# Strassen on part of the last feed-forward product of a decoder layer, with its weight sums made in DRAM

## The chip, the cores and the metric

The kernel runs on one core of one Trainium2 chip. The time is the device time of one launch in microseconds (us). The engines are PE (TensorE: matrix products), ACT (ScalarE), DVE (VectorE), POOL (GpSimd) and SP (SyncE, which here only issues transfers). The core's 16 DMA engines move data between DRAM and the on-chip memory SBUF; matrix products accumulate in PSUM.

## The reference

One decoder layer on 512 tokens of width 1024, in float32, with post-normalisation and a residual weight alpha = 2^0.25:

```python
h = _layernorm(ALPHA * h + 0.5 * _swiglu(h, w_ffn1_in, w_ffn1_out), ln1_g, ln1_b)
h = _layernorm(ALPHA * h + _parallel_mixer(h, w_mix_in, ...), ln2_g, ln2_b)
h = _layernorm(ALPHA * h + _memory_attention(h, mem, xa_wq, xa_wk, xa_wv, xa_wo), ln3_g, ln3_b)
h = _layernorm(ALPHA * h + 0.5 * _swiglu(h, w_ffn2_in, w_ffn2_out), ln4_g, ln4_b)

def _swiglu(h, w_in, w_out):
    gate, up = jnp.split(h @ w_in, 2, axis=-1)
    return (jax.nn.silu(gate) * up) @ w_out
```

The feed-forward width is 2816, so that a second product contracts over 2816 (22 tiles of 128, "k-tiles") and has 512 × 1024 results. The attention has 4 heads and attends to 256 memory tokens.

## The kernel before, in words

**Precision.** Every float32 operand is split into two parts of a shorter type that PE reads faster: ACT copies it into the high half (`split`, L65), DVE subtracts that from the operand and gets the low half (L66). A product is three matmuls: high × high, high × low, low × high.

**Weights.** A weight is read in blocks of 128 × 1024 float32 (512 KB, covering two k-tiles and half of the output columns). `wblock` (L69 to L78) has SP load a block into a buffer `raw_...` (seven of these), ACT cast it into `whi_...`, and DVE make `wlo_...`. Blocks that stay until the end of a product lie in larger buffers `ws_...`.

**Stages.** First feed-forward (f1), the mixer, its output product (mo), the memory keys (weights wk), the memory values (wv, 8 blocks of 12 matmuls, L655 to L671), for each head the queries (wxq, two blocks), scores, softmax and values, the output product of the attention (xo), and the second feed-forward (f2). The first products of the feed-forwards already use Strassen's scheme with seven products (L322). Their second products go through `out_gemm`: for each half of the columns, all 22 k-tiles, four token tiles and three matmuls, 528 in all (L210 to L212, results f2ps, left sides f2gs made from the activations f2g). `ln_tile` then normalises a token tile; POOL computes one column `rstd` for it (L165).

**Order.** A scheduler sets the order within each engine from the order of the program and the buffers; at run time each engine takes its instructions strictly in that order and waits with semaphores. All loads stand in one queue, SP's. POOL has little to do: between the last rstd of mo and the first of xo, nothing.

Of the kernel before, what the change touches and what calls it, by code (L numbers as in the profile page):

```python
# [21 lines left out]
FF = 2816  # L22
FT = FF // P
# [3 lines left out]
ALPHA = 2.0 ** 0.25  # L27
LN_EPS = 1e-5
# [5 lines left out]
def layer_kernel(ctx: ExitStack, tc: tile.TileContext, a, out):  # L34
    nc = tc.nc
# [3 lines left out]
    res = ctx.enter_context(tc.tile_pool(name="res", bufs=1))  # L39
    sm = ctx.enter_context(tc.tile_pool(name="sm", bufs=6))  # L40
    st = ctx.enter_context(tc.tile_pool(name="st", bufs=4))
    psum = ctx.enter_context(tc.tile_pool(name="psum", bufs=6, space=bass.MemoryType.PSUM))

    def b8(shape, dt, name):
        return big.tile(shape, dt, tag="b8", name=name)

    def mm_ps(name):
        return psum.tile([P, 512], F32, tag="mm", name=name)
# [15 lines left out]
    def split(src, hi, lo):  # L64
        nc.scalar.copy(out=hi, in_=src)  # L65
        nc.vector.tensor_tensor(out=lo, in0=src, in1=hi.bitcast(F32), op=ALU.subtract)  # L66


    def wblock(src, name, stay=False):  # L69
        raw = raw4([P, 1024], f"raw_{name}")  # L70
        nc.sync.dma_start(raw, src)
        if stay:
            both = b8([P, 2, 1024], F32R, f"ws_{name}")
            hi, lo = both[:, 0, :], both[:, 1, :]
        else:
            hi, lo = q4([P, 1024], f"whi_{name}"), q4([P, 1024], f"wlo_{name}")
        split(raw, hi, lo)
        return hi, lo  # L78
# [31 lines left out]
    first = [(ps0[0], ps0[1]), (ps0[2], ps0[3])]  # L110
# [17 lines left out]
    xT = [(xt[k // 2][:, k % 2, 0, :], xt[k // 2][:, k % 2, 1, :]) for k in range(KT)]  # L128
# [18 lines left out]
    mhalf = const.tile([P, 4], F32, name="mhalf")  # L147
    nc.vector.memset(mhalf, -0.5)
    h = [res.tile([P, D], F32, name=f"h{t}") for t in range(NT)]


    def ln_bcast(g, b):
        G, B = raw4([P, D], "G"), raw4([P, D], "B")
        nc.sync.dma_start(G, g.partition_broadcast(P))
        nc.sync.dma_start(B, b.partition_broadcast(P))
        return G, B

    def ln_tile(t, stats, GB, eps):
        G, B = GB
        mv = st.tile([P, 2], F32, tag="mv", name="mv")  # L160
        nc.vector.bn_aggr(mv, stats)
        ve = st.tile([P, 1], F32, tag="ve", name="ve")
        nc.vector.tensor_scalar(ve, mv[:, 1:2], eps, None, op0=ALU.add)  # L163
        rstd = st.tile([P, 1], F32, tag="rstd", name="rstd")
        nc.gpsimd.tensor_tensor(out=rstd, in0=ve, in1=mhalf[:, 0:1], op=ALU.pow)  # L165
        for hf in range(2):
            sl = slice(hf * 512, hf * 512 + 512)
            nc.vector.scalar_tensor_tensor(
                out=h[t][:, sl], in0=h[t][:, sl], scalar=mv[:, 0:1], in1=G[:, sl],
                op0=ALU.subtract, op1=ALU.mult)  # L170
            nc.vector.scalar_tensor_tensor(
                out=h[t][:, sl], in0=h[t][:, sl], scalar=rstd, in1=B[:, sl],
                op0=ALU.mult, op1=ALU.add)

    def transpose_h(t, tiles, ys=None):
        if ys is not None:
            if t % 2 == 0:
                ys.append(b8([P, 2, KT, P], F32, f"y{t // 2}"))
        for hf in range(2):
            ps = tr_ps(f"trh{t}{hf}")  # L180
            for j in range(4):
                k = hf * 4 + j
                nc.tensor.transpose(ps[:, j * P:(j + 1) * P], h[t][:, k * P:(k + 1) * P], ident)  # L183
            pv = ps.rearrange("p (a b n) -> p a b n", a=2, b=2)
            for q in range(2):
                T = tiles[hf * 2 + q]
                tsl = slice(t * P, (t + 1) * P)
                split(pv[:, q], T[:, :, 0, tsl], T[:, :, 1, tsl])
            if ys is not None:
                nc.scalar.copy(out=ys[t // 2][:, t % 2, hf * 4:hf * 4 + 4, :], in_=ps.rearrange("p (k n) -> p k n", k=4))  # L190
# [51 lines left out]
        return [(tiles[k // 2][:, k % 2, 0, :], tiles[k // 2][:, k % 2, 1, :]) for k in range(KT)]  # L242


    def proj_T(w, X, n=S, name="pj"):
        hi, lo = w
        ps = mm_ps(name)
        for k in range(KT):
            wsl = slice(k * P, (k + 1) * P)
            mm3(ps[:, :n], hi[:, wsl], lo[:, wsl], X[k][0], X[k][1], k == 0, k == KT - 1)  # L250
        return ps[:, :n]
# [14 lines left out]
    RIGHT = {"a11": "b11", "a12": "b21", "s1": "t1", "s2": "t2", "s3": "t3", "s4": "b22", "a22": "t4"}  # L266
    BANK = {"a11": "u", "s2": "u", "s3": "u", "a22": "u", "s1": "v", "s4": "v", "a12": "w"}

    def ffn(win, wout, xT, todo, g, b, name, final, first=None, lead=2, pre=None, ws0=None):
        gt = [b8([P, 4, S], F32, f"{name}g{q}") for q in range(-(-FT // 4))]  # L270
        raws, quads, ps, sg, c22 = {}, {}, {}, {}, {}
        X = quarters_of(xT)
# [33 lines left out]
        lo, hi = slice(0, 256), slice(256, 512)  # L306
# [60 lines left out]
        for gi in range(0, len(order), 2):  # L367
# [13 lines left out]
            if not final and 4 <= gi < 4 + 2 * NT:  # L381
                t = gi // 2 - 2
                nc.sync.dma_start(h[t], a["x"][t * P:(t + 1) * P, :])
        for j in order[-2:]:
            product(j, "a22")

        gs = {}

        def act(k):
            if k // 2 not in gs:  # L390
# [11 lines left out]
             pre=lambda: wf.extend(wblock(a["wmix"][FF_ + hd], f"wf{hd}") for hd in range(2)))  # L402
# [50 lines left out]
    for hd in range(H):  # L453
        ps = tr_ps("dg")
# [75 lines left out]
    for li, m in enumerate(LEVELS):  # L530
# [6 lines left out]
        for g in range(2):  # L537
            ps = tr_ps(f"lv{m}")
# [49 lines left out]
    for c in range(NT - 1):  # L588
        cs = slice(c * P, (c + 1) * P)
        ps = tr_ps("krt")  # L590
# [24 lines left out]
    for c in range(NT):  # L615
        cs = slice(c * P, (c + 1) * P)
        ps = mm_ps("o")
# [6 lines left out]
        o = sm.tile([P, S], F32, tag="sg", name="o")  # L624
        for hd in range(H):
# [6 lines left out]
                                in0=ps.rearrange("p (h d) -> p h d", h=H),  # L632
                                in1=rs.unsqueeze(2).to_broadcast([P, H, P]), op=ALU.mult)
# [3 lines left out]
    for c, o in enumerate(os_):  # L637
        cs = slice(c * P, (c + 1) * P)
        pt = tr_ps("ot")
        for hd in range(H):  # L640
# [4 lines left out]
            out=og.rearrange("p (h d) -> p h d", h=H), in0=pt.rearrange("p (h d) -> p h d", h=H),  # L645
            scalar=gn[:, 0:1], in1=GS[:, :, cs], op0=ALU.mult, op1=ALU.mult)
# [6 lines left out]

    for k in range(3, KT):
        mem_key(k)  # L655
    VM = [b8([P, 2, D], F32R, f"VM{q}") for q in range(2)]
    for hf in range(2):
        ps = [mm_ps(f"vm{hf}{t}") for t in range(2)]
        for blk in range(4):
            hi, lo = wblock(a["wv"][hf, blk], f"wv{hf}{blk}")  # L660
            for t in range(2):
                tsl = slice(t * P, (t + 1) * P)
                for j in range(2):
                    k = blk * 2 + j
                    wsl = slice(j * 512, (j + 1) * 512)
                    nc.tensor.matmul(ps[t], mT[k][0][:, tsl], hi[:, wsl], start=k == 0, stop=False)
                    nc.tensor.matmul(ps[t], mT[k][0][:, tsl], lo[:, wsl], start=False, stop=False)
                    nc.tensor.matmul(ps[t], mT[k][1][:, tsl], hi[:, wsl], start=False, stop=k == KT - 1)
# [74 lines left out]
    ys, wx = [], []  # L743
    X3 = out_gemm(a["wo"], KT, lambda k: (OT[k // 2][:, k % 2, 0, :], OT[k // 2][:, k % 2, 1, :]),
                  ALPHA, a["ln3_g"], a["ln3_b"], LN_EPS, "xo", ys=ys,
                  pre=lambda: wx.extend(wblock(a["w2in"][u * FT], f"f2{'gu'[u]}0") for u in range(2)))


    ffn(a["w2in"], a["w2out"], X3, lambda: sums_tiles(ys), a["ln4_g"], a["ln4_b"], "f2", True, ws0=wx)


def _cols(w):
# [68 lines left out]
```

## Time and profile before

| | |
|---|---|
| median of three runs | 1080.48 us (1080.31 to 1081.1) |
| the profiled execution's own time | 1082.22 us |
| its span, first to last instruction | 1080.3 us |
| busy: PE / DVE / ACT / POOL | 1066.6 / 732.4 / 456.2 / 40.2 us |
| mean granted PE clock | 0.996 of full speed |
| read from DRAM / written | 110.67 / 2.10 MB |

How to read it: all times within the execution are microseconds from the span's start. A row of a timeline gives the start, the duration, the engine, the line of the code, the operation, the tile written and those read, and the count, with the idle time before it and what ended that in brackets. A row of windows gives the stretch, its length, the busy time and count of each engine, the granted PE clock, the mean busy share of the 16 DMA engines, and GB/s. "PEld" is PE's loading of the stationary operand, which runs beside its matmuls. A row of the list of waits gives the engine and what it wrote, the engine waited for, total us, times and the longest.

### The profile page before, as it was taken

How to read it: one execution, taken by the hardware profiler on the slowest of the kernel's cores; microseconds unless marked ns; L12 is line 12 of the kernel's file. 1: busy time of each engine (PE TensorE's matmuls, PEld its weight loads, DVE VectorE, ACT ScalarE, POOL GpSimd, SP SyncE). 2: the span in 40 equal slices, each digit the busy share in tenths (PEclk: the TensorE clock that was granted, in tenths of full speed). 3: DMA queues.
4: the chain of work that ended last, by engine and by line, in shares of the span. 5: the costliest groups of instructions: out<-in, count | busy, mean ns of one | idle time of the engine just before them, and what ended most of it. 6: DMA issues, size and time to landing. Idle time of an engine off the chain costs nothing. (4 is left out here: it accounts for less than half of the span.)

```text
span 1080.3 us, 17019 instructions
## 1 busy us (share of the span) xinstructions
PE 1066.6 (99%) x6758; PEld 966.0 (89%) x6758; DVE 732.4 (68%) x1316; ACT 456.2 (42%) x810; POOL 40.2 (4%) x54
## 2 busy tenths in 40 slices
PE   9999999999999999999999999999999999999997
PEld 8899999998888888889889988888999999988885
DVE  7999878884425733675777456589987888882516
ACT  5666555572221332223415344335555555561300
POOL 0000000000000020411000000010000000000001
PEclk9999999999999999999999999999999999999999
DMA  9243233263341322222415521301323323443302
GB/s 359 72 136 100 89 111 114 80 188 105 106 139 56 99 62 91 71 80 79 156 39 195 153 82 40 128 29 59 118 79 118 118 79 117 135 124 98 133 1 78
DMA packets 34495, 113.87 MB, mean 105 GB/s; under 512 B 4336, under 2 KB 5616, under 8 KB 34416
## 3 DMA queue, kind: packets, MB, share of 16 engines
q1 hardware_dynamic: 34416, 112.78, 32.3%
q8 instruction: 53, 0.87, 0.3%
q14 instruction: 26, 0.21, 0.1%
HBM read 110.67 MB, written 2.10 MB: 104 GB/s over the span
## 5 line engine op out<-in xcount | busy, mean ns | idle before, releaser
L66 DVE TENSOR_TENSOR wlo_f<-raw_f,whi_f 128x1024 fp32r<-128x1024 f32 x38 | 46.5, 1223 | 85.7 <-PE f1ps L211 39.9
L65 ACT CAST whi_f<-raw_f 128x1024 fp32r<-128x1024 f32 x38 | 40.0, 1052 | 103.1 <-PE f2ps L212 46.5
L322 PE MATMUL f2u<-xt,qf2s 128*128 128x256 f32 x480 | 61.8, 284 | 0.7 <-DVE f2sg L336 0.7
L322 PE MATMUL f1u<-xt,qf1s 128*128 128x256 f32 x480 | 61.5, 284 | 0.0
L322 PEld LDWEIGHTS f2u<-xt,qf2s 128*128 128x128 f32 x480 | 59.1, 192 | 1.9 <-issue 1.9
L322 PEld LDWEIGHTS f1u<-xt,qf1s 128*128 128x128 f32 x480 | 59.4, 193 | 0.4 <-ACT qf1s L65 0.4
L210 PE MATMUL f1ps<-whi_f,f1gs 128*128 128x512 f32 x152 | 59.3, 390 | 0.0
L211 PE MATMUL f1ps<-wlo_f,f1gs 128*128 128x512 f32 x152 | 59.2, 389 | 0.0
L211 PE MATMUL f2ps<-wlo_f,f2gs 128*128 128x512 f32 x152 | 59.2, 389 | 0.0
L210 PE MATMUL f2ps<-whi_f,f2gs 128*128 128x512 f32 x152 | 59.1, 389 | 0.0
L212 PE MATMUL f1ps<-whi_f,f1gs 128*128 128x512 f32 x152 | 59.0, 391 | 0.0
L212 PE MATMUL f2ps<-whi_f,f2gs 128*128 128x512 f32 x152 | 58.8, 390 | 0.0
L165 POOL TENSOR_TENSOR rstd<-ve,mhalf 128x1 f32<-128x1 f32 x16 | 14.4, 900 | 685.4 <-DVE ve L163 685.4
L322 PE MATMUL f1v<-xT,qf1s 128*128 128x256 f32 x240 | 32.2, 291 | 2.1 <-ACT qf1s L65 2.1
L212 PEld LDWEIGHTS f2ps<-whi_f,f2gs 128*128 128x128 f32 x152 | 28.5, 188 | 6.1 <-DVE f2gs L66 0.3
L212 PEld LDWEIGHTS f1ps<-whi_f,f1gs 128*128 128x128 f32 x152 | 28.5, 188 | 6.0 <-DVE f1gs L66 0.3
L211 PEld LDWEIGHTS f2ps<-wlo_f,f2gs 128*128 128x128 f32 x152 | 28.5, 188 | 6.0
L210 PEld LDWEIGHTS f2ps<-whi_f,f2gs 128*128 128x128 f32 x152 | 28.5, 188 | 5.9
L211 PEld LDWEIGHTS f1ps<-wlo_f,f1gs 128*128 128x128 f32 x152 | 28.5, 188 | 5.9
L210 PEld LDWEIGHTS f1ps<-whi_f,f1gs 128*128 128x128 f32 x152 | 28.5, 188 | 5.8
L322 PEld LDWEIGHTS f1v<-xT,qf1s 128*128 128x128 f32 x240 | 30.8, 199 | 2.5 <-ACT qf1s L65 2.3
L322 PE MATMUL f1u<-xT,qf1a 128*128 128x256 f32 x240 | 32.1, 283 | 0.0
(337 smaller groups left out, 2957.1 us busy)
## 6 DMA issues: line engine op xcount, KB each, us to landing
raw_f<-in_w1out SPq DMA_DIRECT2D x22, 512.0 KB, 3.9
raw_f2g<-in_w2in SPq DMA_DIRECT2D x22, 512.0 KB, 3.8
raw_f2u<-in_w2in SPq DMA_DIRECT2D x22, 512.0 KB, 4.1
raw_f<-in_w2out SPq DMA_DIRECT2D x22, 512.0 KB, 3.7
raw_f1g<-in_w1in SPq DMA_DIRECT2D x20, 512.0 KB, 4.1
raw_f1u<-in_w1in SPq DMA_DIRECT2D x20, 512.0 KB, 4.4
raw_wk<-in_wk SPq DMA_DIRECT2D x8, 512.0 KB, 4.6
raw_mo<-in_wmixo SPq DMA_DIRECT2D x8, 512.0 KB, 3.6
```

What stands on the lines that cost most here:

```text
L65: nc.scalar.copy(out=hi, in_=src)
L66: nc.vector.tensor_tensor(out=lo, in0=src, in1=hi.bitcast(F32), op=ALU.subtract)
L165: nc.gpsimd.tensor_tensor(out=rstd, in0=ve, in1=mhalf[:, 0:1], op=ALU.pow)
L210: nc.tensor.matmul(ps[t], ah[:, tsl], wh, start=i == 0 and j == 0, stop=False)
L211: nc.tensor.matmul(ps[t], ah[:, tsl], wl, start=False, stop=False)
L212: nc.tensor.matmul(ps[t], al[:, tsl], wh, start=False, stop=i == nb - 1 and j == 1)
L322: nc.tensor.matmul(o, q[:, w, wsl], x[k][r], start=opens and k == 0 and n == 0, stop=ends and k == 3 and n == 2, skip_group_check=True)
```

## The change

The last feed-forward's second product is computed by another scheme on 16 of its 22 k-tiles. The contraction's first 16 k-tiles and the 1024 columns are cut in two, as are the tokens, and seven products of half sizes stand for eight: 28 blocks × 12 matmuls. The six k-tiles left are done as before (144 matmuls), accumulating into the same PSUM banks. Three of the seven right sides are blocks of the weight itself; four are sums t1 to t4 of blocks. These sums are built in a scratch area of DRAM: for each of four block rows SP issues four DRAM-to-DRAM copies of 512 KB, and POOL four accumulating transfers (t1 += w, t3 += w, t2 += t1, t4 += t2). The calls stand in the loop over the wv blocks, after every second one; a hint puts each copy after SP's latest weight load, and each accumulate after POOL's latest rstd. The left sums are made by DVE from the activations (`combine`).

```diff
+    scr = ctx.enter_context(tc.tile_pool(name="scr", bufs=1, space=bass.MemoryType.DRAM))
...
+    last = [None, None]
     def wblock(src, name, stay=False):
         raw = raw4([P, 1024], f"raw_{name}")
-        nc.sync.dma_start(raw, src)
+        last[0] = nc.sync.dma_start(raw, src).ins
...
-        nc.gpsimd.tensor_tensor(out=rstd, in0=ve, in1=mhalf[:, 0:1], op=ALU.pow)
+        last[1] = nc.gpsimd.tensor_tensor(out=rstd, in0=ve, in1=mhalf[:, 0:1], op=ALU.pow).ins
...
+    class Sums:
+        def __init__(self, wsrc, name):
+            self.w, self.name, self.T, self.todo = wsrc, name, {}, []
+            for b in range(4):
+                for p, hf, kb in (("t1", 0, b), ("t3", 1, b), ("t2", 1, b + 4), ("t4", 0, b + 4)):
+                    self.todo.append((p, b, hf, kb))
+        def copy(self, n):
+            for p, b, hf, kb in self.todo[:n]:
+                T = self.T[p, b] = scr.tile([P, 1024], F32, name=f"{self.name}{p}{b}")
+                with tc.issue_after(last[0]):
+                    nc.sync.dma_start(T, self.w[hf, kb])
+                if p == "t4":
+                    for o, x in (("t1", self.w[1, b]), ("t3", self.w[1, b + 4]), ("t2", self.T["t1", b]), ("t4", self.T["t2", b])):
+                        with tc.issue_after(last[1]):
+                            nc.gpsimd.dma_start(self.T[o, b], x, accum_op=ALU.add, max_dma_last_dim=8192)
+            del self.todo[:n]
+
+    def strassen_gemm(wsrc, gt, S_, alpha, g, b, eps, name, final, pre):
...
+        def left(p):
+            T = []
+            for i in range(2):
+                t = b8([P, 4, 2, 256], F32R, f"{name}{p}{i}")
+                split(quarter_[p][i], t[:, :, 0, :], t[:, :, 1, :])
+                T.append(t)
+            return T
+        def combine(o, x, y, op):
+            for i in range(2):
+                nc.vector.tensor_tensor(out=quarter_[o][i], in0=quarter_[x][i], in1=quarter_[y][i], op=op)
+        def right(p):
+            direct = {"b11": (0, 0), "b21": (0, 4), "b22": (1, 4)}
+            for i in range(4):
+                src = wsrc[direct[p][0], direct[p][1] + i] if p in direct else S_.T[p, i]
+                yield wblock(src, f"{name}{p}{i}")
+        def product(T, p, ps, opens, ends):
+            for i, (wh, wl) in enumerate(right(p)):
+                for j in range(2):
+                    k = 2 * i + j
+                    csl = slice(j * 512, (j + 1) * 512)
+                    for t in range(2):
+                        tsl = slice(t * P, (t + 1) * P)
+                        ah, al = T[k // 4][:, k % 4, 0, tsl], T[k // 4][:, k % 4, 1, tsl]
+                        for n, (x, y) in enumerate(((ah, wh), (ah, wl), (al, wh))):
+                            nc.tensor.matmul(ps[t], x, y[:, csl], ...)
...
+        L = left("a11")
+        product(L, "b11", u, True, False)
+        combine("s1", "a21", "a22", ALU.subtract)
+        L = left("s1")
...   (products t1, t2, b21, t3, b22, t4 in the same manner, with their additions into h)
+        ws = [[wblock(wsrc[hf, kb], f"{name}{hf}_{kb}", stay=hf == 0 or kb < 10) for kb in range(8, FT // 2)]
+              for hf in range(2)]
...
+        if sums_out is not None:
+            return strassen_gemm(wout, gt, sums_out, 2.0 * ALPHA, g, b, 4.0 * LN_EPS, name, final, pre)
...
+    sums2 = Sums(a["w2out"], "f2")
     for hf in range(2):
         ps = [mm_ps(f"vm{hf}{t}") for t in range(2)]
         for blk in range(4):
             hi, lo = wblock(a["wv"][hf, blk], f"wv{hf}{blk}")
+            if blk % 2 == 1:
+                sums2.copy(4)
...
-    ffn(a["w2in"], a["w2out"], X3, lambda: sums_tiles(ys), a["ln4_g"], a["ln4_b"], "f2", True, ws0=wx)
+    ffn(a["w2in"], a["w2out"], X3, lambda: sums_tiles(ys), a["ln4_g"], a["ln4_b"], "f2", True, ws0=wx,
+        sums_out=sums2)
```

SP's queue at the wv blocks (raw_wv00 is the first block, raw_wxq00 the first query block). Before, and then of the change:

```order
138 L71 DMA raw_wv00_5650<-in_wv 128x1024
139 L71 DMA raw_wv01_5668<-in_wv 128x1024
140 L71 DMA raw_wv02_5686<-in_wv 128x1024
141 L71 DMA raw_wv03_5704<-in_wv 128x1024
142 L71 DMA raw_wv10_5728<-in_wv 128x1024
```

```order
L74 DMA raw_wv02_5700<-in_wv 128x1024
L74 DMA raw_wv03_5718<-in_wv 128x1024
L261 DMA f2t11_5724<-in_w2out 16x8192
L261 DMA f2t31_5726<-in_w2out 16x8192
L261 DMA f2t21_5728<-in_w2out 16x8192
L261 DMA f2t41_5730<-in_w2out 16x8192
L74 DMA raw_wv10_5754<-in_wv 128x1024
L74 DMA raw_wv11_5772<-in_wv 128x1024
L261 DMA f2t12_5778<-in_w2out 16x8192
```

Four copies now stand behind each second wv block, and so four ahead of the third, fifth and seventh wv block and the first query block.

POOL's queue from the last rstd of mo on (f2t10 is the sum t1 of the first block row). Before, and then of the change:

```order
48 L165 TENSOR_TENSOR rstd_5457<-ve_5455,mhalf_260 128x1
49 L165 TENSOR_TENSOR rstd_6644<-ve_6642,mhalf_260 128x1
```

```order
L168 TENSOR_TENSOR rstd_5459<-ve_5457,mhalf_262 128x1
L265 DMA f2t10_5676<-in_w2out 64x2048
L265 DMA f2t30_5678<-in_w2out 64x2048
L265 DMA f2t20_5680<-f2t10_5676 64x2048
L265 DMA f2t11_5724<-in_w2out 64x2048
L265 DMA f2t31_5726<-in_w2out 64x2048
L265 DMA f2t40_5682<-f2t20_5680 64x2048
L265 DMA f2t21_5728<-f2t11_5724 64x2048
L265 DMA f2t41_5730<-f2t21_5728 64x2048
```

The 16 accumulates stand between the last rstd of mo and the first of xo, where nothing stood.

PE's queue at the start of the last product (f2gs0 and f2a110 are the first left sides, u0 and u1 two token tiles). Before, and then of the change:

```order
2855 L210 MATMUL f2ps00_9617<-whi_f20_0_9613,f2gs0_9618 128x512
2856 L211 MATMUL f2ps00_9617<-wlo_f20_0_9614,f2gs0_9618 128x512
2857 L210 MATMUL f2ps01_9627<-whi_f20_0_9613,f2gs0_9618 128x512
2858 L211 MATMUL f2ps01_9627<-wlo_f20_0_9614,f2gs0_9618 128x512
2861 L210 MATMUL f2ps03_9641<-whi_f20_0_9613,f2gs0_9618 128x512
2862 L211 MATMUL f2ps03_9641<-wlo_f20_0_9614,f2gs0_9618 128x512
2863 L212 MATMUL f2ps00_9617<-whi_f20_0_9613,f2gs0_9618 128x512
```

```order
2855 L303 MATMUL f2u0_9661<-whi_f2b110_9676,f2a110_9667 128x512
2856 L303 MATMUL f2u0_9661<-wlo_f2b110_9677,f2a110_9667 128x512
2857 L303 MATMUL f2u1_9662<-whi_f2b110_9676,f2a110_9667 128x512
2858 L303 MATMUL f2u1_9662<-wlo_f2b110_9677,f2a110_9667 128x512
2859 L303 MATMUL f2u0_9661<-whi_f2b110_9676,f2a110_9667 128x512
2860 L303 MATMUL f2u1_9662<-whi_f2b110_9676,f2a110_9667 128x512
```

A matmul that reads the low half of the left side is the third of its kind on a token tile (L212, and the second `whi` row of u0): it is now the fifth of the product, where it was the ninth.

More of the change, by code (lines that the diff above doesn't have):

```diff
@@ new lines, in strassen_gemm, with add @@
+    def strassen_gemm(wsrc, gt, S_, alpha, g, b, eps, name, final, pre):
+        tiles = None
+        stats = [st.tile([P, 2, 6], F32, tag=f"stats{t}", name=f"stats{t}", bufs=1) for t in range(NT)]
+        lo, hi = slice(0, 256), slice(256, 512)
+        quarter_ = {"a11": [gt[0][:, :, lo], gt[1][:, :, lo]], "a12": [gt[2][:, :, lo], gt[3][:, :, lo]],
+                    "a21": [gt[0][:, :, hi], gt[1][:, :, hi]], "a22": [gt[2][:, :, hi], gt[3][:, :, hi]]}
+        def left(p):
[22 more added lines that the diff above has]
+                        for n, (x, y) in enumerate(((ah, wh), (ah, wl), (al, wh))):
+                            nc.tensor.matmul(ps[t], x, y[:, csl], start=opens and k == 0 and n == 0,
+                                             stop=ends and k == 7 and n == 2, skip_group_check=True)
+        def add(t, hf, ps, scale, op=ALU.add):
+            sl = slice(hf * 512, hf * 512 + 512)
+            if scale:
+                nc.vector.scalar_tensor_tensor(out=h[t][:, sl], in0=h[t][:, sl], scalar=float(alpha), in1=ps,
+                                               op0=ALU.mult, op1=op)
+            else:
+                nc.vector.tensor_tensor(out=h[t][:, sl], in0=h[t][:, sl], in1=ps, op=op)
+        u, v, w = ([mm_ps(f"{name}{n}{t}") for t in range(2)] for n in "uvw")
+        L = left("a11")
+        quarter_["s1"] = [x for x in [b8([P, 2, 4, 256], F32, f"{name}s1")] for x in (x[:, 0], x[:, 1])]
+        product(L, "b11", u, True, False)
+        combine("s1", "a21", "a22", ALU.subtract)
+        L = left("s1")
+        for t in range(2):
+            add(t, 0, u[t], True)
+        product(L, "t1", v, True, False)
+        combine("a21", "a11", "a21", ALU.subtract)
+        combine("a11", "s1", "a11", ALU.subtract)
+        L = left("a11")
+        for t in range(2):
+            add(2 + t, 1, v[t], True)
+        product(L, "t2", u, False, False)
+        L = left("a12")
+        for t in range(2):
+            add(t, 1, u[t], True, ALU.subtract)
+        product(L, "b21", w, True, False)
+        combine("a12", "a12", "a11", ALU.add)
+        L = left("a21")
+        gs = {}
+        for k in range(16, FT, 2):
+            T = gs[k // 2] = b8([P, 2, 2, S], F32R, f"{name}gs{k // 2}")
+            split(gt[k // 4][:, k % 4:k % 4 + 2, :], T[:, :, 0, :], T[:, :, 1, :])
+        product(L, "t3", u, False, False)
+        L = left("a12")
+        for t in range(2):
+            add(2 + t, 1, u[t], False, ALU.subtract)
+        product(L, "b22", v, False, False)
+        L = left("a22")
+        product(L, "t4", u, False, False)
+        ws = [[wblock(wsrc[hf, kb], f"{name}{hf}_{kb}", stay=hf == 0 or kb < 10) for kb in range(8, FT // 2)]
+              for hf in range(2)]
+        GB = ln_bcast(g, b)
+        if pre is not None:
+            pre()
+        for t in range(NT):
+            tsl = slice(t * P, (t + 1) * P)
+            for hf in range(2):
+                if t < 2:
+                    ps = (w, v)[hf][t]
+                else:
+                    ps = u[t - 2] if hf == 0 else mm_ps(f"{name}x{t}")
+                for i, (wh, wl) in enumerate(ws[hf]):
+                    for j in range(2):
+                        csl = slice(j * 512, (j + 1) * 512)
+                        ah, al = gs[8 + i][:, j, 0, tsl], gs[8 + i][:, j, 1, tsl]
+                        for n, (x, y) in enumerate(((ah, wh), (ah, wl), (al, wh))):
+                            nc.tensor.matmul(ps, x, y[:, csl], start=t >= 2 and hf == 1 and i == 0 and j == 0 and n == 0,
+                                             stop=i == 2 and j == 1 and n == 2, skip_group_check=True)
+                add(t, hf, ps, t >= 2 and hf == 0)
+                nc.vector.bn_stats(stats[t][:, hf, :], h[t][:, hf * 512:hf * 512 + 512])
+            ln_tile(t, stats[t], GB, eps)
+            if final:
+                for q in range(2):
+                    nc.sync.dma_start(out[t * P:(t + 1) * P, q * 512:(q + 1) * 512], h[t][:, q * 512:(q + 1) * 512])
+            else:
+                if t == 0:
+                    tiles = [b8([P, 2, 2, S], F32R, f"{name}T{q}") for q in range(4)]
+                transpose_h(t, tiles)
+        if final:
+            return None
+        return [(tiles[k // 2][:, k % 2, 0, :], tiles[k // 2][:, k % 2, 1, :]) for k in range(KT)]
@@ L267, in layer_kernel, with ffn @@
     BANK = {"a11": "u", "s2": "u", "s3": "u", "a22": "u", "s1": "v", "s4": "v", "a12": "w"}
-    def ffn(win, wout, xT, todo, g, b, name, final, first=None, lead=2, pre=None, ws0=None):
+    def ffn(win, wout, xT, todo, g, b, name, final, first=None, lead=2, pre=None, ws0=None, sums_out=None):
         gt = [b8([P, 4, S], F32, f"{name}g{q}") for q in range(-(-FT // 4))]
```

## The prediction

> **What bounds the kernel now.** First the page's busy shares and the list of waits, then windows by stage for the DMA share and the clock, then single rows around the places that the change touches.
>
> ```profile
> PE 1066.6 (99%) x6758; PEld 966.0 (89%) x6758; DVE 732.4 (68%) x1316; ACT 456.2 (42%) x810; POOL 40.2 (4%) x54
> PE f1v L322 <- ACT qf1s L65: 2.1, 1, 2.1
> ```
>
> TensorE (PE) is busy for 1066.6 of 1080.3 us and its longest wait for another engine is 2.1 us. Whatever takes matmuls away is gained in full, and whatever makes PE wait is lost in full, because there is no slack to eat it. So two stages decide: the last product, where matmuls go, and the value and query projections of the attention, where 16 copies and 16 accumulating transfers are put in.
>
> ```profile
> 953.00:1073.00 120.00, 119.79 (x528) 98.65 (x526) 4.97 (x8) 1.00 0.24 79
> 569.00:584.00 15.00, 15.00 (x126) 14.87 (x125) 13.19 (x25) 7.59 (x15) 0.98 (x1) 1.00 0.62 211
> 584.00:606.00 22.00, 22.00 (x101) 18.28 (x100) 12.23 (x13) 10.59 (x13) 0.00 (x0) 1.00 0.66 198
> 606.00:674.00 68.00, 67.76 (x403) 59.89 (x403) 36.03 (x71) 30.02 (x65) 0.00 (x0) 1.00 0.24 76
> 16.00:20.00 4.00, 4.00 (x19) 3.30 (x19) 2.15 (x4) 1.89 (x4) 0.00 (x0) 1.00 1.02 409
> ```
>
> The first row is of the tile f2ps alone (window; PE, weight loads, DVE; clock, DMA share, GB/s), the others are of all work (PE, weight loads, DVE, ACT, POOL; clock, DMA share, GB/s). The second and third rows are the key: from 569 to 606 PE has no gap at all and the 16 DMA engines are already taken for 0.62 to 0.66 of the time, while from 606 to 674 they are at 0.24. The room for transfers lies behind 606, and the transfers are put ahead of it.
>
> **The matmuls.** The f2ps row gives 119.79 / 528 = 0.2269 us for a matmul. The new code runs 7 products of 48 and 6 k-tiles of 24: 336 + 144 = 480. 48 × 0.2269 = **10.9 us** removed, all on the path. The loads go from 22 to 34 blocks of 512 KB in the same stage, so the DMA share of 0.24 in that row becomes about 0.24 × 34/22 = 0.37: no new bound.
>
> **The start of the product.** PE's order (shown with the change) has 8 matmuls with the high half of the activations before, then one with the low half; after, 4 and then two.
>
> ```profile
> 952.79 0.40 PE L210 MATMUL f2ps<-whi_f,f2gs 128*128 128x512 f32 x1
> 953.36 5.76 DVE L66 TENSOR_TENSOR f2gs<-f2g,f2gs 128x1024 fp32r<-128x1024 f32 x5
> 954.63 0.50 PE L212 MATMUL f2ps<-whi_f,f2gs 128*128 128x512 f32 x1
> L212 PEld LDWEIGHTS f2ps<-whi_f,f2gs 128*128 128x128 f32 x152 | 28.5, 188 | 6.1 <-DVE f2gs L66 0.3
> ```
>
> The first low half is a 1024-wide DVE operation from 953.36, and PE took it up at 954.63, having waited 0.3 us already. With 4 matmuls in front, PE arrives at 952.79 + 4 × 0.23 = 953.7 and waits 0.9 us; 0.3 of it is in the time before. Cost: **+0.65 us**.
>
> **DVE in the seven products.** Every weight block needs one 1024-wide low half (28), each left side two (14), the last three activation pairs one each (3), each of the four left sums two (8): 53 operations, and 8 additions into h.
>
> ```profile
> L66 DVE TENSOR_TENSOR wlo_f<-raw_f,whi_f 128x1024 fp32r<-128x1024 f32 x38 | 46.5, 1223 | 85.7 <-PE f1ps L211 39.9
> L65 ACT CAST whi_f<-raw_f 128x1024 fp32r<-128x1024 f32 x38 | 40.0, 1052 | 103.1 <-PE f2ps L212 46.5
> L227 DVE SCALAR_TENSOR_TENSOR h<-h,f2ps 128x512 f32<-128x512 f32 x8 | 5.5, 686 | 19.8 <-PE f2ps L212 19.8
> ```
>
> 53 × 1.22 + 8 × 0.69 = 70 us of DVE beside 336 × 0.2269 = 76 us of PE, or 92%. ACT has 45 casts × 1.05 = 47 us. It fits, but tightly: laying the DVE order against the products by these durations, DVE is just in time at the fifth product, after the three activation pairs. Bounds: 0, and 6 us if each of the seven products waits for most of one operation. I take **+0.8 us**, near the low end, since the sum leaves 6 us free.
>
> **The transfers ahead of the value and query weights.** By SP's order (shown with the change) the 16 copies stand in fours behind the second, fourth, sixth and eighth wv block; POOL's 16 accumulating transfers stand behind the last rstd of the norm before.
>
> ```profile
> 543.24 1.56 SPq L71 DMA_DIRECT2D raw_wv<-in_wv  x2
> 569.57 0.33 SPq L71 DMA_DIRECT2D raw_wv<-in_wv  x1
> 573.47 1.68 SPq L71 DMA_DIRECT2D raw_wv<-in_wv  x2
> 582.19 0.33 SPq L71 DMA_DIRECT2D raw_wxq<-in_wq  x1
> raw_wv<-in_wv SPq DMA_DIRECT2D x8, 512.0 KB, 4.4
> 597.51 1.06 ACT L65 CAST whi_wxq<-raw_wxq 128x1024 fp32r<-128x1024 f32 x1 [1.18 <-PE vm L668]
> 600.06 1.23 DVE L66 TENSOR_TENSOR wlo_wxq<-raw_wxq,whi_wxq 128x1024 fp32r<-128x1024 f32 x1 [1.50 <-PE vm L667]
> 605.47 0.28 PE L54 MATMUL pxq<-moT,whi_wxq 128*128 128x256 f32 x1
> 573.54 0.98 POOL L165 TENSOR_TENSOR rstd<-ve,mhalf 128x1 f32<-128x1 f32 x1 [9.08 <-DVE ve L163]
> ```
>
> Copies 1 to 4 cost nothing: SP has the first two wv blocks out by 544.8 and its next load at 569.57, so they lie in idle time. Copies 5 to 16 stand in the queue ahead of wv blocks 5 and 7 and the first wxq block. The rstd starts at 573.54, so the accumulates begin at about 574.5: in the same 30 us.
>
> When must the first wxq block be there? Its first matmul is at 605.47 and its third, 0.24 us later, needs the low half: 605.71 − 1.23 − 1.06 − 0.2 for hand-overs = 603.2. When will it be? Work on the engines in front of it, from the end of the fourth wv block's issue at 573.8: 12 copies (c each), the loads of four wv blocks and its own, and the accumulates let in between (n of a each). A 512 KB load takes 0.524 MB / 409 GB/s × 1.02 = 1.31 us of all 16 engines (the 16:20 row); it lands 4.4 us after issue, so 3.1 us are fixed. It lands at 573.8 + 3.1 + 5 × 1.31 + 12c + n·a = 583.45 + 12c + n·a.
>
> No transfer from DRAM to DRAM is in the trace. The nearest rows are the load and, for writing DRAM, the last two stores (window 1076:1081):
>
> ```profile
> q1 hardware_dynamic: 288, 0.52, 28.3%
> out<-h SPq DMA_DIRECT2D x2, 256.0 KB, 2.0
> ```
>
> 0.283 × 5 us = 1.42 us for 512 KB. Bounds of c: 1.31 (a copy is one transfer, as the load is) to 1.31 + 1.42 = 2.73 (both ends in DRAM). Bounds of a: 1.31 to two reads and a write, 4.04. Both kinds are as near to one row as to the other, so I take the middles, c = 2.0 and a = 2.7. For n: none if accumulates do not get in; 10 if they keep up with the copies (groups 1 to 3 have 12, and the last ones wait in turn for two landings); I take 7, since each step of their chain must wait for a landing (2.0 us for a store) beside its own transfer.
>
> - Low end: 583.45 + 15.7 = 599.2, before 603.2: no wait (with n = 4, 604.4 and 1.2 us).
> - Taken: 583.45 + 24.0 + 18.9 = 626.4: **+23.1 us**.
> - High end: 583.45 + 32.8 + 40.4 = 656.6: +53.4 us.
>
> SP is also held back: it has eight transfers in flight, each new one waiting for the eighth before it, so wv block 7 and the wxq blocks wait for copies to land; that stretches the same queue and adds no term. Queued behind a late wxq block are its cast on ACT and low half on DVE, and PE behind those.
>
> The Trainium skill bears on both unknowns. "DMA: Bandwidth & Descriptors", section "Latency and other measured facts", gives 207 to 214 GB/s per direction for copies between HBM tensors; by it a copy is an estimated 2.45 us, the block lands at 631.8 and the wait is 28.6 us. Its section "Issuing engines are not separate DMA queues" says that transfers started by POOL and by SP run on the same 16 engines and interleave, so that POOL's queue buys no room; no run here shows two queues at once, and without that sharing the n·a term would go and the wait would be 4.3 us.
>
> **The clock.** After the one 2.1 us wait of PE the granted clock falls:
>
> ```profile
> 36.00:40.00 4.00, 1.92 (x12) 1.31 (x10) 4.00 (x5) 3.38 (x7) 0.00 (x0) 1.00 0.00 0
> 40.00:44.00 4.00, 3.98 (x23) 3.78 (x23) 4.00 (x8) 2.63 (x6) 0.00 (x0) 0.66 0.37 100
> 44.00:48.00 4.00, 4.00 (x33) 4.00 (x32) 2.35 (x6) 2.53 (x5) 0.00 (x0) 0.92 0.43 168
> ```
>
> (1 − 0.66) × 4 + (1 − 0.92) × 4 = 1.7 us for one wait. Here there will be one long wait or two or three: 1.7 to 5; I take **+2.5 us**.
>
> **POOL's other work.** What POOL owes next is the rstd of the layer norm behind attention:
>
> ```profile
> 707.00 0.91 POOL L165 TENSOR_TENSOR rstd<-ve,mhalf 128x1 f32<-128x1 f32 x1 [132.47 <-DVE ve L163]
> ```
>
> It now stands behind 16 transfers, of which some ten must wait for one another. They have 707.0 − 574.5 = 132.5 us, 13.2 for a step; a landing of 2.0 and a transfer of 2.7 make 4.7. Cost 0, covered by 132 us of attention.
>
> **Sum.** The profiled execution took 1082.22 us: 1082.2 − 10.9 + 0.65 + 0.8 + 23.1 + 2.5 = 1098.4. The median of the runs is 1.74 lower (1080.48): 1096.6, **about 1097 us**, slower by 1.5%.
>
> **Rivals.**
> 1. *The transfers fit (faster).* Mechanism: the engines take a copy at the speed of a load and the accumulates get in seldom, so the first wxq block lands before 603.2. For it: the low end above, and 34 to 38% of free DMA time in the stage. Against: 12 copies alone use 15.7 us even then, where 569 to 606 had 37 × 0.36 = 13 us free. Time: 1082.2 − 10.9 + 1.45 − 1.74 = **1071**. It decides as long as wait and clock together stay below 9.4 us; below 7.3 the kernel is measurably faster, above 11.6 measurably slower (0.2%, 2.2 us, is what a measurement can tell from no change). Between lies a half-hidden pile-up that comes out at about 1080.5.
> 2. *DVE becomes the bound of the seven products.* For it: 92% by the sum. Against: 6 us free. It would add up to 5 us: 1076 with hidden transfers, 1102 with the pile-up.
> 3. *POOL is late.* If a step takes over 13.2 us, PE waits for the norm; at 16 us the last accumulate ends at 734.5, 27.5 us late: 1082.2 − 10.9 + 1.45 + 27.5 + 1.7 − 1.74 = 1100. Against: 4.7 us by the rows.
>
> That the change does not do what it says can be left out: 480 matmuls follow from the code.
>
> **Chances.** Pile-up 0.60; transfers fit 0.22 (0.02 of it within 0.2%); half hidden 0.08; DVE bound alone 0.05 (0.01 of it within 0.2%); POOL late 0.05. Faster 0.20 + 0.04 = 0.24, same 0.02 + 0.08 + 0.01 = 0.11, slower 0.65. Low end of the range: 1082.2 − 10.9 + 0.65 − 1.74 = 1070. High end: the wait's bound of 53.4 would give 1127 to 1132, which needs every unknown at its worst; 1118, a wait of some 44 us, leaves about 0.1 above. The pile-up's own range is 1083 to 1118.
>
> **What would show it.** In the changed kernel: landing times of wv and wxq blocks several times 4.4 us; PE waits between 595 and 640 whose releasers are casts or low halves of wxq, behind a transfer; a DMA share near 1 from 574 to beyond 606; clock rows below 1 behind the waits; the last product 109 to 111 us long; POOL's rstd of the attention's norm no later than PE's own delay. I am wrong if PE stays busy through 606, or if it waits in the last product for more than 3 us, or if wxq lands in time while something else is late.

## The result, and the profile after

The changed kernel takes 1095.26 us (median of four runs, 1094.7 to 1096.53) against 1080.79 us for the kernel before on the same chip: ratio **1.0134**, interval 1.0117 to 1.0152. It is slower by 14.5 us. The forecast was 1097.

The page's busy shares, and the DMA queues of the changed kernel (packets, MB moved, share of the 16 engines' time):

```profile
PE 1061.7 (97%) x6710; PEld 960.4 (88%) x6710; DVE 766.2 (70%) x1350; ACT 473.4 (43%) x828; POOL 53.4 (5%) x70
q1 hardware_dynamic: 36656, 127.47, 35.4%
q0 software_dynamic: 1280, 8.39, 3.9%
```

PE works 4.9 us less than before, and the span is longer: 1092.9 us against 1080.3. A second DMA queue, q0, carries POOL's accumulates. The list of PE's waits says where the time went:

```profile
PE vm L807 <- ACT whi_wv L66: 10.3, 1, 10.3
PE pxq L55 <- ACT whi_wxq L66: 5.7, 1, 5.7
PE f1v L458 <- ACT qf1s L66: 2.1, 1, 2.1
...
PE f2u L303 <- DVE f2a L67: 0.7, 1, 0.7
PE vm L808 <- DVE wlo_wv L67: 0.5, 1, 0.5
PE pxq L57 <- DVE wlo_wxq L67: 0.5, 1, 0.5
```

The value product (vm) and the first query product (pxq) wait 10.3 + 5.7 + 0.5 + 0.5 = 17.0 us. ACT's timeline shows that the casts named as releasers themselves waited for transfers, and the windows (PE, weight loads, DVE, ACT, POOL; clock, DMA share, GB/s) that the DMA engines were full:

```profile
609.29 1.04 ACT L66 CAST whi_wv<-raw_wv 128x1024 fp32r<-128x1024 f32 x1 [13.83 <-DMA raw_wv<-in_wv]
624.26 1.04 ACT L66 CAST whi_wxq<-raw_wxq 128x1024 fp32r<-128x1024 f32 x1 [9.87 <-DMA raw_wxq<-in_wq]
```

```profile
569.00:584.00 15.00, 15.00 (x125) 14.87 (x124) 13.18 (x25) 7.59 (x15) 2.74 (x3) 1.00 0.77 234
584.00:606.00 22.00, 16.10 (x71) 12.97 (x70) 5.56 (x6) 3.70 (x5) 3.92 (x5) 0.94 1.00 283
606.00:640.00 34.00, 22.96 (x122) 20.17 (x123) 9.77 (x11) 9.21 (x12) 5.55 (x7) 0.74 1.03 320
```

From 584 to 640 the 16 DMA engines are full (shares of 1.00 and 1.03), where 0.66 and less of them was in use before. The median landing (from issue to arrival) of a wv block went from 4.4 to 9.5 us, and of a query block from 4.3 to 20.2. The last column is this median:

```profile
f2t<-in_w2out SPq DMA_DIRECT2D x16, 512.0 KB, 14.6
raw_wv<-in_wv SPq DMA_DIRECT2D x8, 512.0 KB, 9.5
raw_wxq<-in_wq SPq DMA_DIRECT2D x8, 512.0 KB, 20.2
```

Two marks bound the loss and the gain. POOL's first rstd behind attention stood at 707.00 and now stands here:

```profile
653.21 0.78 POOL L265 DMA_DIRECT2D f2t<-f2t  x1 [7.19 <-DMA f2t<-f2t]
729.94 0.93 POOL L168 TENSOR_TENSOR rstd<-ve,mhalf 128x1 f32<-128x1 f32 x1 [75.95 <-DVE ve L166]
```

It is 22.9 us later: 17.0 us of waits, and a rest of 5.9 us that is put down to a lower clock (the windows at the end of this text give about 5.5 us for it). (The last accumulate is issued at 653.21, 76 us before POOL is needed.) The last product's first and last matmul:

```profile
975.09 0.40 PE L303 MATMUL f2u<-whi_f2b,f2a 128*128 128x512 f32 x1
976.93 0.98 PE L303 MATMUL f2u<-whi_f2b,f2a 128*128 128x512 f32 x3 [0.74 <-DVE f2a L67]
1084.77 0.39 PE L364 MATMUL f2x<-whi_f,f2gs 128*128 128x512 f32 x1
```

It starts 22.3 us later than before (952.79) and ends 12.4 us later (1072.40): a gain of 9.9 us, with one wait of 0.74 us at its start.

### The profile page after: what moved, and what is told of

It reads as the page before. It is cut to its first block, busy times and chain, and to the rows that moved or that the text cites. A ratio compares the mean times of both kernels' runs of the same rounds, so it can differ in the third digit from the quotient of the medians.

```text
span 1092.9 us, 17081 instructions
## 1 busy us (share of the span) xinstructions
PE 1061.7 (97%) x6710; PEld 960.4 (88%) x6710; DVE 766.2 (70%) x1350; ACT 473.4 (43%) x828; POOL 53.4 (5%) x70
## 5 line engine op out<-in xcount | busy, mean ns | idle before, releaser
L67 DVE TENSOR_TENSOR wlo_f<-raw_f,whi_f 128x1024 fp32r<-128x1024 f32 x20 | 24.4, 1222 | 42.8 <-PE f1ps L214 39.9
L66 ACT CAST whi_f<-raw_f 128x1024 fp32r<-128x1024 f32 x20 | 21.1, 1053 | 51.2 <-PE f1ps L215 46.0
L67 DVE TENSOR_TENSOR wlo_wv<-raw_wv,whi_wv 128x1024 fp32r<-128x1024 f32 x12 | 14.7, 1225 | 39.6 <-ACT whi_wv L66 22.0
L55 PE MATMUL pxq<-moT,whi_wxq 128*128 128x512 f32 (+1 forms) x80 | 28.8, 360 | 5.7 <-ACT whi_wxq L66 5.7
L458 PE MATMUL f1w<-xT,qf1a 128*128 128x256 f32 x240 | 32.1, 283 | 0.0
L458 PE MATMUL f2w<-xoT,qf2a 128*128 128x256 f32 x240 | 32.1, 283 | 0.0
L458 PE MATMUL f2u<-xoT,qf2a 128*128 128x256 f32 x240 | 32.0, 283 | 0.0
L437 DVE TENSOR_TENSOR f2s<-raw_f2u 128x512 f32<-128x512 f32 x20 | 13.8, 691 | 25.7 <-DMA raw_f2u<-in_w2in 25.7
```

Source lines behind the costliest of these rows:

```text
L55: nc.tensor.matmul(o, lh, rh, start=first, stop=False)
L437: nc.vector.tensor_tensor(out=s1, in0=a21, in1=a22, op=ALU.subtract)
L458: nc.tensor.matmul(o, q[:, w, wsl], x[k][r], start=opens and k == 0 and n == 0, stop=ends and k == 3 and n == 2, skip_group_check=True)
```

## The experiments

Theory: the copies and accumulates together take more of the DMA engines than is free before the first query block is due at 603.2; neither kind alone does. Four runs test it against the rivals, and with them the place of the transfers.

**Copies without accumulates.** The four accumulates of each group are left out; products t1 to t4 multiply by plain weight blocks in place of sums.

```diff
-                if p == "t4":
-                    for o, x in (...):
-                        with tc.issue_after(last[1]):
-                            nc.gpsimd.dma_start(self.T[o, b], x, accum_op=ALU.add, max_dma_last_dim=8192)
```

> The changed kernel without its 16 accumulating transfers; the copies stay where they are, so four of the seven products use plain weight blocks in place of sums. In the changed kernel's trace the first four copies, which run alone, took 1.34 us of the DMA engines each, and the accumulates 2.65 us. Theory (the sum of both kinds exceeds what the engines have free before the first query block is due): without the accumulates the block lands at 583.45 + 12 x 1.34 = 599.5, before 603.2, PE does not wait, and the time is the kernel before less 10 us: about 1071. Rival A (the copies alone do it, because the weight blocks queue behind them in SP's queue and SP holds eight transfers at most): two waits of PE remain, 15 us or more with the clock's part: about 1086.

Measured: 1070.95 us, ratio 0.9912 (0.9896 to 0.9929). PE has no wait in the value and query products; in this run's window and ACT's timeline:

```profile
569.00:606.00 37.00, 37.00 (x225) 33.15 (x224) 24.03 (x36) 16.69 (x26) 0.98 (x1) 1.00 0.90 345
602.22 1.05 ACT L66 CAST whi_wxq<-raw_wxq 128x1024 fp32r<-128x1024 f32 x1 [5.75 <-DMA raw_wxq<-in_wq]
```

The cast of the first query block began at 602.2, where a landing at 599.5 had been expected and 603.2 was the limit. Rival A falls: the copies alone, queue and all, cost nothing, though the margin is thin.

**Copies early.** All 16 copies stand behind the second wv block, where SP is idle.

```diff
-            if blk % 2 == 1:
-                sums2.copy(4)
+            if hf == 0 and blk == 1:
+                sums2.copy(16)
```

> The changed kernel with all 16 copies put behind the second wv block, where SP idles from 545 to 569; the accumulates stand where they stood. 16 x 1.34 = 21.4 us, so the copies are done by about 567. Theory: what is left beside the loads is the accumulates alone, a load gets half of the engines at worst and lands within 8 us instead of 4.4, which the loads' lead of 15 to 20 us covers: no wait over 1 us, about 1071. Rival B (the accumulates alone do it, POOL's queue taking half of the engines for as long as it has work): PE waits for wv or query blocks, 8 us or more, about 1080.

Measured: 1077.03 us, ratio 0.9973 (0.9962 to 0.9984): between the two expected times. PE's waits, and the queues' shares of the engines from 576 to 606:

```profile
PE pxq L55 <- ACT whi_wxq L66: 2.3, 1, 2.3
...
PE pxq L57 <- DVE wlo_wxq L67: 1.5, 2, 0.8
...
PE vm L808 <- DVE wlo_wv L67: 0.8, 1, 0.8
```

```profile
q0 software_dynamic: 689, 4.60, 74.9%
q1 hardware_dynamic: 813, 2.96, 26.7%
```

The expectation that a load keeps half of the engines was wrong. POOL's accumulates had three quarters, and query blocks took 29.3 us to land. So the accumulates alone do cause waits (4.6 us), less than rival B asked, and by a cause that the theory lacked: how the two queues share. The theory's "neither kind alone" holds for the copies only.

**Copies late.** All 16 copies stand behind the last query block.

```diff
-            if blk % 2 == 1:
-                sums2.copy(4)
...
     xq(3)
+    sums2.copy(16)
     p1 = attend(1)
```

> The changed kernel with all 16 copies moved behind the last query block in SP's queue; the accumulates wait for them by data, so all 32 transfers run from about 602 on. Theory: nothing stands ahead of the value and query blocks, PE does not wait there; 16 x 1.34 + 16 x 2.65 = 64 us of the engines fit into 602 to 707, where 0.24 of them are in use. POOL's chain of ten steps, 6 to 10 us each as in the changed kernel, ends by 665 to 705, before the rstd at 707: about 1071. If a step takes over 10.5 us, POOL is late for the rstd and the time rises by what it is late. Rival A or B: also about 1071, so this run tests the remedy, not the split.

Measured: 1079.97 us, ratio 0.9995 (0.9984 to 1.0006): no difference from the kernel before. The waits in value and query products are gone, as expected, and POOL is in time. But the next loads in the queue, the blocks of the attention's output product, became late; the list of waits and the timeline show what followed:

```profile
ACT whi_xo L66 <- DMA raw_xo<-in_wo: 15.0, 2, 11.9
...
PE po L55 <- ACT PT L66: 5.6, 2, 5.4
```

```profile
648.54 1.04 ACT L66 CAST whi_xo<-raw_xo 128x1024 fp32r<-128x1024 f32 x1 [11.88 <-DMA raw_xo<-in_wo]
649.97 1.08 ACT L66 CAST PT<-pt 128x512 fp32r<-128x512 f32 x2
682.02 0.40 PE L213 MATMUL xops<-whi_xo,oT 128*128 128x512 f32 x1
```

ACT takes its instructions in order: its cast of an xo block, which PE uses only at 682.02, waited 11.9 us for its transfer, and behind it stood the cast of the softmax weights (PT), for which PE waited 5.4 us. The pile-up was moved, not removed: POOL's first rstd behind attention starts at 714.71, 7.7 us later than in the kernel before, which takes back most of what the new product gains.

**No sums.** Neither copies nor accumulates; products t1 to t4 read plain weight blocks.

```diff
-                src = wsrc[direct[p][0], direct[p][1] + i] if p in direct else S_.T[p, i]
+                hf, kb = direct[p] if p in direct else {"t1": (0, 0), "t2": (1, 4), "t3": (1, 0), "t4": (0, 4)}[p]
+                src = wsrc[hf, kb + i]
...
-            if blk % 2 == 1:
-                sums2.copy(4)
```

> The changed kernel without any copies or accumulates: the four products that want sums use plain weight blocks instead, so the last product has its 480 matmuls and its DVE work but no sums are made. Theory: the whole loss lies in the transfers during attention, and the last product gains 48 matmuls x 0.2269 = 10.9 us less 0.74 us at its start (as in the changed kernel's trace): ratio 0.9906, about 1070.7. Rival C (the new product itself has waits that the changed kernel's late clock hides or makes): 1075 or more.

Measured: 1069.86 us, ratio 0.9906 (0.9891 to 0.9921). The product alone gains 10.0 us; rival C falls.

**How the queues share.** The early copies opened a question. One answer: the queues take turns packet by packet, so that the queue with the longer packets gets the larger share. Four of the next five runs change the sizes of packets, two of them with the copies early; one undoes the new product. First, the changed kernel with accumulates in rows of 2 KB:

```diff
-    nc.gpsimd.dma_start(self.T[o, b], x, accum_op=ALU.add, max_dma_last_dim=8192)
+    nc.gpsimd.dma_start(self.T[o, b], x, accum_op=ALU.add, max_dma_last_dim=2048)
```

> The changed kernel with the accumulates cut into rows of 2 KB in place of 8 KB; nothing else. In the changed kernel POOL's queue and SP's queue each had about half of the engines (47.9% and 52.6% from 574 to 625), where SP's copies and POOL's accumulates both took about 0.66 us for a packet of one engine (2.65 us x 16 / 64 and 1.34 us x 16 / 32); with the early copies SP had only loads (4 KB, 1.31 us x 16 / 128 = 0.16 us for a packet) and got 0.31 against 0.71. Theory D (the two queues take turns packet by packet, so that the larger packets get the larger share): at 2 KB an accumulate's packet takes 0.165 us, SP's queue gets 0.8, the first query block lands at about 573.8 + 3.1 + 22.7 / 0.8 = 605, PE waits 2 to 4 us in place of 17, and the time is about 1075. Rival E (the engines are shared by bytes or by halves whatever the packets): no change, about 1095; if 2 KB rows cost more time a byte, slower still.

Measured: 1082.35 us, ratio 1.0019 (1.001 to 1.0028). The shares from 574 to 606, in the changed kernel and then in this run:

```profile
q1 hardware_dynamic: 839, 6.34, 53.4%
q0 software_dynamic: 425, 2.85, 46.2%
```

```profile
q1 hardware_dynamic: 1069, 8.78, 71.7%
q0 software_dynamic: 916, 1.78, 32.7%
```

It is 2.3 us slower than the kernel before on its chip, where the change was 14.5 us slower: 12.2 us are back by the row size alone, so rival E falls. But the expected 1075 was missed by 7 us: SP's queue rose from 0.53 to 0.72, not to 0.8; the query block was cast at 611.9, not 605, and PE still waited 4.0 + 1.2 + 0.8 + 0.5 us. One figure of the expectation was also wrong: a copy's 32 packets are not alike. In every run a transfer has 16 packets more than rows (an accumulate 80 for 64 rows of 8 KB, 272 for 256 rows of 2 KB), so a copy has 16 long ones, its rows of 32 KB, of about 1.34 us each, and 16 very short ones; 0.66 us is their mean.

**Early copies and accumulates of 2 KB**, both edits together:

> Copies early (behind the second wv block) and accumulates of 2 KB rows. Theory D: a load's packet and an accumulate's take the same 0.165 us, SP gets half of the engines instead of the 0.31 of the early copies alone; the loads need 0.65 of them, so they fall behind by about 0.15 x 30 = 5 us, which their lead covers: no wait of PE over 0.5 us, about 1071. Rival E: as with the early copies alone, 1077.

Measured: **1070.54 us, ratio 0.9912 (0.9896 to 0.9929)**, and this kernel leaves nothing out. It is faster than with either edit alone. No wait is left in the value and query products; its shares from 576 to 606 and its windows:

```profile
q0 software_dynamic: 1582, 3.07, 55.7%
q1 hardware_dynamic: 1545, 5.64, 51.0%
```

```profile
574.00:606.00 32.00, 32.00 (x183) 28.14 (x182) 20.50 (x26) 16.15 (x23) 7.18 (x8) 1.00 1.05 291
606.00:640.00 34.00, 34.00 (x204) 30.40 (x203) 13.04 (x22) 11.46 (x20) 6.24 (x7) 1.00 1.09 264
```

The engines are as full as in the changed kernel, and PE never stops. What counts is whose packets get through, not that the engines are busy.

**Copies in rows of 4 KB**, accumulates as in the change (8 KB):

```diff
-                    nc.sync.dma_start(T, self.w[hf, kb])
+                    nc.sync.dma_start(T, self.w[hf, kb], max_dma_last_dim=4096)
```

> The changed kernel with the 16 copies cut into rows of 4 KB in place of 32 KB, the accumulates as they were. Theory D: SP's packets are then 0.16 us against 0.66, SP's queue gets 0.2 to 0.3 of the engines as long as POOL has work; up to 12 or 14 accumulates go ahead of the first query block, which lands at 573.8 + 3.1 + 22.7 + 12 to 14 x 2.65 = 631 to 637 instead of 624: PE waits 6 to 12 us longer, about 1101 to 1107. Rival E: no change, about 1095.

Measured: 1098.53 us, ratio 1.017 (1.0155 to 1.0185), against 1.0134 for the change: slower, in the expected direction and by less. From 574 to 606 SP's queue fell from 0.53 to 0.45, not to 0.3, and the first query block was cast at 628.8, in place of 624.3 (a landing at 631 or later was expected). The expected share was there while POOL had work: from 588 to 604, SP's queue had 24.8% and POOL's 76.0%. But POOL's accumulates wait for copies and for one another to land, and from 604 to 612 its queue had 21.7% and SP's 83.2%. Those pauses are what the expectation left out.

**The transfers with the old product.** The 32 transfers stay, and the last product is the one before.

```diff
-    ffn(..., ws0=wx,
-        sums_out=sums2)
+    ffn(..., ws0=wx)
```

> The kernel before with the 32 transfers of the change, and with its own last product (528 matmuls; the sums are made and not used). Theory: gain and loss are two places that do not touch each other; the transfers cost what they cost in the changed kernel, 17 us of waits and 5 to 6 us of lower clock: 1080 + 22.5 = about 1102.5, and with the 10 us that the product alone gained (1069.9 against 1079.9) the parts add up to the changed kernel's +14. Rival F (part of the 22 us comes from the new product's own loads or order): 1095 or less.

Measured: 1103.82 us, ratio 1.0218 (1.0199 to 1.0237), +23.8 us. With the product's −10.0 us the parts add up to +13.7; the change measured +14.5. Rival F falls.

**The size between.** Early copies, accumulates in rows of 4 KB:

```diff
-    nc.gpsimd.dma_start(self.T[o, b], x, accum_op=ALU.add, max_dma_last_dim=8192)
+    nc.gpsimd.dma_start(self.T[o, b], x, accum_op=ALU.add, max_dma_last_dim=4096)
```

> Copies early, accumulates in rows of 4 KB: the size between the two already run. From 576 to 606 SP's queue, with loads alone, had 0.267 of the engines against 0.749 with 8 KB rows, and 0.510 against 0.557 with 2 KB rows. Theory D (turns packet by packet): an accumulate's packet of 4 KB takes 2.65 x 16 / 128 = 0.33 us against a load's 0.16, so SP's queue gets 0.33 to 0.38; the query blocks' landing lies between the 29.3 us and the 10.0 us of the two, about 16 us, PE waits 0 to 2 us in all, and the time is 1070.5 to 1074. Rival G (the gain at 2 KB came from the smaller rows being slower or later as such, or from their longer issue on POOL, not from the turns): the share of 8 KB, 0.27, and about 1077.

Measured: 1070.02 us, ratio 0.99 (0.988 to 0.992), no wait in the stage. Shares from 576 to 606:

```profile
q0 software_dynamic: 1046, 3.83, 64.3%
q1 hardware_dynamic: 1216, 4.44, 40.0%
```

With loads of 4 KB in SP's queue, its share was 0.27, 0.40 and 0.51 for accumulates of 8, 4 and 2 KB, and the query blocks' median landing 29.3, 21.0 and 10.0 us. Rival G falls. The expected 0.33 to 0.38 is met once both queues have work (36.5% from 580 to 604, shown at the end); from 576 to 580 the accumulates had only begun. At 4 KB a landing of 21 us is already covered by the loads' lead.

## Why the prediction was right, point by point

**The matmuls and the start of the product.** 10.9 us less 0.65 and 0.8 was forecast, 9.45; the trace shows 9.9 and the run without sums 10.0. The wait at the start was 0.74 us (0.65 above what was there before, by the forecast). The 0.8 us for DVE in the seven products was not there: PE's only wait for another engine between the product's first and last matmul is that 0.74 us. Rival 2 is out.

**The pile-up.** The mechanism and the place of the waits were as forecast. Of the three sizes in its sum, one was right, and the other two were wrong in opposite directions.

- c, a copy: 2.0 us taken, 1.31 to 2.73 bounded. The first four copies ran without accumulates, beside two loads: from 543 to 560 q1 was busy for 50.4% of 17 us, in the kernel before for 18.8%:

```profile
q1 hardware_dynamic: 416, 3.15, 50.4%
```

```profile
q1 hardware_dynamic: 288, 1.05, 18.8%
```

(8.57 − 3.20) / 4 = 1.34 us, like a load. The low bound was the right row; taking the middle put 12 × 0.66 = 7.9 us too much into the term. The figure of 207 to 214 GB/s in the Trainium skill, "DMA: Bandwidth & Descriptors", section "Latency and other measured facts", given there for rows of 16 KiB that lie far apart and from which 2.45 us was estimated, does not hold for these contiguous copies: 0.524 MB in 1.34 us are 391 GB/s, and the measurement decides.
- a, an accumulate: 2.7 us taken. From 574 to 665, which holds all 16, q0 was busy for 46.4% of 91 us:

```profile
q0 software_dynamic: 1280, 8.39, 46.4%
```

42.2 / 16 = 2.64 us: right.
- n, the accumulates that get in: 7 taken. By 625, q0 had moved 4.82 MB, 9.2 accumulates: 5.8 us too little in the term.

583.45 + 12 × 1.34 + 9.2 × 2.64 = 623.8, and the query block was cast at 624.26; 626.4 was forecast. The two errors, 7.9 us and 5.8 us, nearly cancel. That was luck: the total was better than its parts.

**Waits and clock.** 23.1 + 2.5 = 25.6 us were forecast for the two together, 22.9 came: 17.0 of waits and 5.9 of lower clock. The clock was the mis-sized term. The forecast also added the block's whole lateness as a wait; but PE does the vm matmuls behind its first wait, at 612 to 620, with a clock of 0.50 and 0.87 (shown below), and that work is part of the lateness. So part of what was called wait was lost as clock. That SP's hold on wv block 7 "adds no term" was right for the total, but the larger of the two waits, 10.3 us, was at that block.

**The rivals.** Rival 1 (the transfers fit) would have been the result without the accumulates: c was at its low end, as that rival said, but the accumulates did get in. The argument held against it, that 12 copies need 15.7 us where 13 were free, was a misreading: in the run with copies alone they fitted. Of the 23.8 us of engine time that was taken from 569 to 606 in the kernel before (37 us less the 13 free), the forecast's own sum counts only five blocks, 6.6 us, ahead of the deadline; loads that are due later can give way. Rival 3 (POOL late) is out by 76 us. The sum against the profiled execution was 1098.4; that execution took 1094.7.

**What the forecast lacked.** It treated the engines as one ring in which only total work counts. The row size alone took the time from 1077 to 1070 us with the copies early, and from 1095 to 1082 with the copies in place, for the same bytes, at no lower cost (an accumulate took 2.67 us of the engines in rows of 4 KB and 2.87 in rows of 2 KB, by q0's shares of the whole span, 4.0% and 4.3%). The sharing rule of the Trainium skill quoted in the forecast ("Issuing engines are not separate DMA queues") agrees with every run here: q0 and q1 together never make more than 1.07 of the 16 engines in the stretches shown.

## What to carry to other kernels

A stage's DMA headroom has to be counted up to the moment at which the next needed block is due, with the transfers ahead of it in its own queue and the share that other queues take; a mean over the stage hides this. Background transfers belong in a stretch where the loading queue is idle, and those of another queue should have packets no longer than those of the loads that they run beside. A load that is late can also stop work that does not need it, through an engine that takes its instructions in order.

## What the runs showed of the hardware

**Shares by packet.** Two queues on the same 16 engines did not share by halves. They took turns, one packet each. This shows in the counts of packets while both queues had work, from 580 to 604 with the copies early; accumulate rows of 8, 4 and 2 KB beside loads of 4 KB:

```profile
q0 software_dynamic: 599, 3.89, 78.2%
q1 hardware_dynamic: 607, 2.22, 24.6%
```

```profile
q0 software_dynamic: 895, 3.27, 68.3%
q1 hardware_dynamic: 897, 3.28, 36.5%
```

```profile
q0 software_dynamic: 1279, 2.46, 55.3%
q1 hardware_dynamic: 1280, 4.67, 52.1%
```

The counts agree to 1.4% or better, whatever the rows. So the shares follow the durations of the packets: SP's share over POOL's is 0.31, 0.53 and 0.94, where 0.164 us for a load's packet over 0.66, 0.33 and 0.18 us for an accumulate's gives an estimated 0.25, 0.50 and 0.91. The changed kernel does the same: from 592 to 600, with copies in SP's queue, there were 121 packets of SP's and 122 of POOL's. By turns, a copy's long and short packet together (1.34 us) stand against two of the accumulate's (1.32 us); this gives the halves, 46.8% and 53.1%, in that stretch. Over a longer stretch the shares are less clear-cut, since POOL's queue is not always full: each accumulate that reads a sum waits for the one before it.

**A copy from DRAM to DRAM** costs the engines about as much as a load (1.34 against 1.31 us for 512 KB), an accumulate in rows of 8 KB twice as much (2.64).

**The clock behind a wait.** Windows of the changed kernel:

```profile
604.00:608.00 4.00, 0.00 (x0) 0.00 (x0) 0.00 (x0) 0.00 (x0) 0.41 (x1) 0.50 1.04 262
608.00:612.00 4.00, 1.15 (x2) 0.65 (x3) 1.64 (x2) 1.53 (x2) 0.00 (x0) 0.50 1.06 316
612.00:616.00 4.00, 4.00 (x10) 3.11 (x10) 1.42 (x2) 1.04 (x1) 2.30 (x3) 0.50 0.95 382
616.00:620.00 4.00, 3.64 (x14) 2.58 (x12) 0.00 (x0) 0.00 (x0) 0.08 (x1) 0.87 1.05 301
620.00:624.00 4.00, 0.00 (x0) 0.00 (x0) 0.00 (x0) 0.00 (x0) 0.00 (x0) 0.98 1.02 248
624.00:628.00 4.00, 2.17 (x8) 1.88 (x9) 1.82 (x2) 1.53 (x2) 0.78 (x1) 0.50 0.98 259
628.00:632.00 4.00, 4.00 (x26) 4.00 (x25) 2.32 (x3) 2.48 (x3) 0.00 (x0) 0.67 1.06 337
```

The granted clock falls to 0.50 within a wait (in the second one only behind 620 to 624, a row without any work that still shows 0.98) and stays there for at least 4 us of work behind it: 10 matmuls from 612 to 616, where 0.2269 us for each would make 17 or 18. PE's busy time in each row times what its clock lacks of 1 adds up to about 5.5 us, near the 5.9 left over above. So two waits of 10.3 and 5.7 us cost 5 to 6 us more in this way, where the one wait of 2.1 us in the kernel before had cost 1.7.
